# A streaming encoder step: sums of squares a k-tile per place, later first queries, four cosine buffers, w_out tiles written early, and rows of the second pair in another order

## The chip, the cores and the metric

The kernel runs on one core of one Trainium2 chip. The metric is the device time of one execution in microseconds, and the median over the runs is what counts. The engines are PE (matmul, with PEld for its weight loads), DVE (vector), ACT (scalar, with tables for functions such as Exp), POOL, and SP, which here only issues transfers.

## The reference

One inference step of a one-layer encoder on 2048 frames of a new stream and 64 frames of a running one, all in float32:

```
xn = rmsnorm(x, norm_mix);  proj = xn @ w_in              # 1024 -> 5632
x_rnn, y_gate, q, k, v, g_rnn, g_attn = split(proj)
xc = causal_dwconv(x_rnn);  h = rg_lru(xc)                # gates, then a scan over the frames
y_rnn = h * gelu(y_gate)
y_attn = window attention(rope(q), rope(k), v, sinks)     # 16 heads, 4 key heads, chunks of 64
x = x + (sigmoid(g_rnn)*y_rnn + sigmoid(g_attn)*y_attn) @ w_out
up = rmsnorm(x, norm_ffn) @ w_up;  gate, val = split(causal_dwconv(up))
x = x + (silu(gate) * val) @ w_down;  y = rmsnorm(x, norm_final)
```

Caches (keys, values, the recurrent state and the last rows of both convolutions) are outputs too.

## The kernel before

Channels lie on partitions and the 2112 tokens (2048 and 64) along the free dimension. A float32 product is made of three matmuls on a high and a low part of each operand (`mm3`, L237 to L239: `xh` and `xl` against the weight pair `whl`). `split` (L204, L205) makes such a pair: ACT rounds to the high part, then DVE subtracts for the low part, so the low part waits for ACT. `split2` and `put2` (L209, L210) do the same and return the low part as a call to be made later.

**Phase 1** (to about 1350 us) works on three sets of two token blocks (320, 384 and 352 columns a block). A set goes through the 44 tiles of w_in, 48 matmuls a tile (8 k-tiles, 3 parts, 2 blocks), into three PSUM banks in turn. In set 0, `kept` loads a tile as plain float32 (`wraw`, 512 KB, issued by SP at L226), splits it into `whl`, and POOL writes the pair to DRAM (`wiS`); sets 1 and 2 load the pairs. `wraw` has two slots and, through `fw.extend`, a third in a region `FX`.

A set begins with the projections of the queries and then of the keys, each followed by `rope` for either block (L375 to L381 on DVE, which read two PSUM banks). `trig` (L395, L396) loads the cosines and sines of a block into tiles named `h`, two of them. The results go to DRAM (`qS`, `kS`), from where attention reads them. Four groups follow, one per key head. In a group, `rnn` goes through 18 places (j = 0 to 17) of projections, gates, scan and gelu for two channel tiles (conv L623 and L628, gates L652 to L655, gelu's eviction L688, L699 to L721), and at each place one step of `attention` is taken beside it: a unit loads its queries (D and E, L539), makes scores S (L547, L548), a softmax (L550 to L565, Exp on ACT at L559), transposes `pt` of the probabilities with their split into `ph` and `pl`, and the product Y (L580, L581).

The next set's input norm is made beside groups 2 and 3 of a set. `stats` loads 8 k-tiles for each of two blocks (L255), squares them on ACT (L257, L259) and adds them up on POOL (L260); `finish` later sums over partitions with a matmul. Both blocks' 16 loads and squares are written at one place, g = 2, j = 8. `behind()` places what is written in it behind the last weight load.

**Phase 2** (to about 1565 us) multiplies by w_out for three pairs of blocks. `wload` loads 48 half tiles: the first 16 raw, the rest as pairs that were kept in DRAM (`RE<-woS`, L438). `mixes` loads the operands of the next pair (`FW<-mixS`, L411), through SP too. **Phases 3 and 4** are the feed-forward, with seven products in place of eight for each 2 by 2 square of quarters; ORDER lists the products' operands. `x1prep` makes the operands T1, 21 and 22 of the second pair from x after phase 2 (loads L909, scale L916, difference L925, then `put2`). It runs as one of the things taken beside the products. Where a quarter's product is ready, L1206 and L1208 add it up out of PSUM on DVE, which frees the bank.

Until `tc.manual_schedule()` (in front of phase 3) a scheduler chooses the order of the instructions on each engine; behind it the order is the one written.

Of the kernel before, what the change touches and what calls it, by code (L numbers as in the profile page):

```python
# [7 lines left out]
F32 = mybir.dt.float32  # L8
F32R = mybir.dt.float32r
AF = mybir.ActivationFunctionType  # L10
ALU = mybir.AluOpType
# [3 lines left out]
P = 128  # L15
T = 2112
TP = 2048
KO = 8
# [3 lines left out]
SETS = [[(0, 320), (320, 320)], [(640, 384), (1024, 384)], [(1408, 352), (1760, 352)]]  # L22
BN = 384
# [103 lines left out]
def kernel(ctx: ExitStack, tc: tile.TileContext, xT, w_in, w_out, w_up, w_dn, gw, pk,  # L127
                             sinks, cq, sq, ck, sk, kcT, vcT, kcn, vcn, augk, auge, ident_in,
                             yT, kpT, ksT, vpT, vsT, kc_o, vc_o, h_o, lc_o, fc_o):
    nc = tc.nc  # L130
# [116 lines left out]
        xblocks[t0] = (pool.tile([P, KO, BN], F32R, name="xh", bufs=2), pool.tile([P, KO, BN], F32R, name="xl", bufs=2))  # L247
        return xblocks[t0]

    def stats(t0, n):  # L250
        r = fw.tile([P, BN], F32, name="nr", bufs=2)[:, :n]
        s = fw.tile([P, BN], F32, name="ns", bufs=2)[:, :n]
        for k in range(KO):
            x = fw.tile([P, BN], F32, name="xk", bufs=4)[:, :n]
            nc.sync.dma_start(x, xT[k * P:(k + 1) * P, t0:t0 + n])  # L255
            if k == 0:
                nc.scalar.activation(s, x, AF.Square)  # L257
            else:
                nc.scalar.activation(x, x, AF.Square)  # L259
                nc.gpsimd.tensor_tensor(s, s, x, op=ALU.add)  # L260

        def finish():
            p = pmm.tile([P, 512], F32, name="mm")
            nc.tensor.matmul(p[:, :n], ones, s, start=True, stop=True)
            nc.scalar.activation(r, p[:, :n], AF.Sqrt, scale=1.0 / 1024, bias=epst)
            nc.vector.reciprocal(r, r)
            rstd[t0] = r
        return finish

    def apply(blocks):  # L270

# [67 lines left out]
        consts()  # L339

    es1 = ExitStack()

    FX = Region(tc, "FX", 4096, F32, "right")
    es1.callback(FX.close)
    fw.regions = (FW, FX)
    fw.extend("wraw", KO * P, 1)
    ap = es1.enter_context(tc.tile_pool(name="ap", bufs=1, reuse_waits="tile", side="right"))
    rp_ = es1.enter_context(tc.tile_pool(name="rp", bufs=2, reuse_waits="tile", side="right"))
    pat = es1.enter_context(tc.tile_pool(name="pat", bufs=1, space=PSUM))
# [40 lines left out]
            nc.sync.dma_start(qS[i, r0:r0 + 128, tt], t[:, :n].bitcast(F32))  # L390

    def trig(c, s, r, tt, n):
        ct = rp_.tile([P, BN], F32, name="h")
        st = rp_.tile([P, BN], F32, name="h")
        nc.sync.dma_start(ct[:r, :n], c[:, tt])  # L395
        nc.sync.dma_start(st[:r, :n], s[:, tt])  # L396
        return ct, st
# [33 lines left out]
    def wload(j):  # L431

        if j < 16:
            wraws[j] = raws.tile([P, 4 * P], F32, name="wraw")
            nc.sync.dma_start(wraws[j], w_out[j // 2][:, j % 2 * 4 * P:(j % 2 + 1) * 4 * P])
        elif j < 48:
            weights[j] = wh.tile([P, 2, 4 * P], F32R, name="wh")
            nc.sync.dma_start(weights[j].bitcast(F32), wpart(j))  # L438
# [12 lines left out]
    for si, blocks in enumerate(SETS):  # L451
# [285 lines left out]
        for g in range(4):  # L737
            kv = key_prep(g)
            ya = ap.tile([P, 2, SN], F32, name="ya")
            rr = [rp_.tile([P, SN], F32, name=f"rr{i}", bufs=1) for i in range(2)]  # L740
            ta = [[], []]
            at = attention(g, kv)
            for j, _ in enumerate(rnn(g, rr, ta)):
                next(at, None)
                if j == 3:
                    while pending:
                        pending.pop(0)()
                if g == 2 and j == 8 and si + 1 < len(SETS):
                    with behind():
                        nxt = [stats(t0, n) for t0, n in SETS[si + 1]]  # L750
                if g == 3 and j == 6:
                    for f in nxt:
                        f()
                if g == 3 and nxt:

                    if j == (16 if si == 0 else 8):
                        ahead = apply(SETS[si + 1])
                    if j in ((16, 17) if si == 0 else (9, 13, 15)):
                        with behind():
                            next(ahead)  # L760
            if g == 3 and nxt:
                for _ in ahead:
                    pass
            if g == 1 and si == 2:

                fw.close()
                xk, raws = Pool(FW), Pool(FW, right=True)
                xk.reserve("xk", BS, 16)
                raws.reserve("wraw", 4 * P, 2)
                mixed = mixes(0, xk)  # L770
                with behind():
                    next(mixed)
                    wload(0)
                    wload(1)
            if g == 3 and si == 2:

                es0.close()
                RA = Region(tc, "RA", 58368, F32R)
                mixp, wh0 = [Pool(RA), None, None], Pool(RA)
                wh0.reserve("wh", 8 * P, 4)  # L780
            for _ in at:
                if g == 3 and si == 2:
                    next(mixed)
                    next(mixed)
                    next(mixed)
            for i in range(2):
                pending.append(lambda i=i, rr=rr, ta=ta, ya=ya, g=g, blocks=blocks, s0=s0:
                               mix(2 * g + i, rr[i], ta[i], ya[:, i], blocks, s0))
# [107 lines left out]
    def x1prep(p, rs, tp):  # L896

        (t0, n), (t1, _) = PAIRS[p]
        for o in ("T1", "21", "22"):
            operand(p, o)  # L900
        where = {"11": (0, t0), "12": (0, t1), "21": (4, t0), "22": (4, t1)}
        todo = [(o, k) for k in range(4) for o in ("12", "11")] + [(o, k) for o in ("21", "22") for k in range(4)]
        raw, low = [], []

        def load(j):
            if j < len(todo):
                half, t = where[todo[j][0]]
                raw.append(tp.tile([P, n], F32, name="x1", bufs=8))
                nc.sync.dma_start(raw[j], x1S[todo[j][1] + half, :, t:t + n])  # L909

        for j in range(8):
            load(j)
        yield
        for j, (o, k) in enumerate(todo):
            half, t = where[o]
            nc.vector.scalar_tensor_tensor(raw[j], raw[j], col("g2", k + half), rs[t], op0=ALU.mult, op1=ALU.mult)  # L916
            while low:
                low.pop(0)()
                load(len(raw))
                if j < 10:  # L920
                    load(len(raw))
            if o == "12":
                continue
            if o == "11":
                nc.vector.tensor_tensor(raw[j], raw[j - 1], raw[j], op=ALU.subtract)  # L925
                o = "T1"
            low.append(put2(p, o, k, raw[j]))
            yield
        low.pop()()
# [16 lines left out]
    def wout(i, m, beside):  # L946

        work = [(t0, n, xres.pop((t0, m)), acc()) for t0, n in phases[i]]
        for j in (16 * i + 2 * m, 16 * i + 2 * m + 1):
# [9 lines left out]
                    nc.tensor.matmul(ps[:, :n], w[:, 1, c], x[:, k, 0], start=False, stop=k == 7)  # L959
            wsplit(j + 2)  # L960
            while wnext[0] < 48 and wnext[0] <= j + 4:
                wload(wnext[0])
                wnext[0] += 1
            beside()
        return work
# [430 lines left out]
    for i in range(3):  # L1396
# [14 lines left out]
        for m in range(8):  # L1411
# [17 lines left out]
            if i == 0 and m == 5:  # L1429
                drive(side, 99)  # L1430
                xk.close()
                xk = Pool(FW, right=True)
                xk.reserve("xk", BM, 3)
                side, pace = [mixes(2, xk)], (1, 0)
# [437 lines left out]
```

## Time and profile before

| | us |
|---|---|
| median of 3 runs | 2969.44 |
| lowest and highest | 2962.66, 2976.83 |
| profiled execution | 2964.2 |
| its span | 2962.4 |
| mean granted clock of PE | 0.983 |

Times in the profile are counted from the start of the span. A row of the time line has the start, the length, engine, line, operation, tiles (out<-in) and, in brackets, how long the engine had been idle and what released it. Where the prediction speaks of a wait of PE, it is such a bracket.

### The profile page before, as it was taken

Reading aid. Unit: us, or ns where it says so; the run is one execution under the profiler, and the core shown is the slowest. Engines: PE = TensorE matmul, PEld = TensorE weight load, DVE = VectorE, ACT = ScalarE, POOL = GpSimd, SP = SyncE. Lnnn points to the kernel's source line nnn. Section 1 sums busy time; section 2 is a strip of 40 time slices with the busy share of each in tenths; the row PEclk is TensorE's granted clock in tenths of the full one; section 3 lists DMA queues with packets and bytes.
Section 4 is the critical chain, followed back from the end, with each engine's and each line's share of the span. In section 5 each row is a group of like instructions: output and inputs, shape, how many; then the busy total and the mean of one; then the engine's idle time right before and its main releaser. Section 6 shows DMA issues by size and latency. Waiting matters only on the chain.

```text
span 2962.4 us, 48650 instructions
## 1 busy us (share of the span) xinstructions
PE 2856.2 (96%) x17572; PEld 2749.1 (93%) x17572; DVE 2037.4 (69%) x3998; ACT 1507.7 (51%) x3353; POOL 400.6 (14%) x699
## 2 busy tenths in 40 slices
PE   7999899999999999998898999999899999999998
PEld 6899899999999999998898999999799999999997
DVE  6388784467686277776567988888756557656686
ACT  4377772466654266665324555555544444333442
POOL 2012100000200000002321323333111111000011
PEclk8999999999999999999999999999999999999999
DMA  7867656644455745436875656565766666977573
GB/s 250 282 210 229 193 198 226 193 149 135 152 162 169 244 141 182 147 125 247 274 234 178 219 195 220 200 221 201 259 202 219 215 223 210 278 208 223 162 231 112
DMA packets 337042, 601.13 MB, mean 203 GB/s; under 512 B 39216, under 2 KB 236832, under 8 KB 319904
## 3 DMA queue, kind: packets, MB, share of 16 engines
q1 hardware_dynamic: 288096, 409.28, 44.9%
q0 software_dynamic: 48704, 188.73, 16.8%
q8 instruction: 139, 2.28, 0.3%
q14 instruction: 103, 0.84, 0.1%
HBM read 398.11 MB, written 200.29 MB: 202 GB/s over the span
## 4 chain that ended last, share of the span: by engine, by line
PE 61%; issue 15%; DVE 10%; DMA 8%; ACT 3%; POOL 2%; SPq 0%; POOLq 0%; DVEq 0%; ACTq 0%
PE mm L237 9%; PE mm L239 9%; PE mm L238 9%; PE mf L1157 3%; PE mf L1159 3%; PE mf L1158 3%; PE mf L1678 2%; PE mf L1677 2%; PE mf L1679 2%; DMA x1S<-FW 2%; PE mm L1159 2%; PE mm L1157 2%; PE mm L1158 2%; PE pt L572 2%; DMA FW<-in_xT_dram 1%
## 5 line engine op out<-in xcount | busy, mean ns | idle before, releaser
L237 PE MATMUL mm<-xh,whl 128*128 128x320 f32 (+2 forms) x2112 | 691.1, 327 | 12.6 <-DVE y L379 9.6
L238 PE MATMUL mm<-xl,whl 128*128 128x320 f32 (+2 forms) x2112 | 687.2, 325 | 5.4 <-DVE xl L205 4.7
L239 PE MATMUL mm<-xh,whl 128*128 128x320 f32 (+2 forms) x2112 | 685.9, 325 | 0.0
L209 ACT ACTIVATE RE<-FW 128x512 fp32r<-128x512 f32 (+2 forms) x540 | 288.0, 559 | 398.9 <-DVE FW L1036 98.2
L210 DVE TENSOR_TENSOR RE<-FW,RE 128x512 fp32r<-128x512 f32 (+2 forms) x540 | 313.4, 602 | 161.1 <-ACT RE L209 156.1
L237 PEld LDWEIGHTS mm<-xh,whl 128*128 128x128 f32 x2112 | 401.7, 190 | 19.7 <-DVE y L379 11.1
L238 PEld LDWEIGHTS mm<-xl,whl 128*128 128x128 f32 x2112 | 401.8, 190 | 12.2 <-DVE xl L205 8.0
L239 PEld LDWEIGHTS mm<-xh,whl 128*128 128x128 f32 x2112 | 401.4, 190 | 0.8
L1193 DVE SCALAR_TENSOR_TENSOR FA<-FA,pkt 128x608 f32<-128x608 f32 (+1 forms) x264 | 245.4, 950 | 51.1 <-ACT FA L1187 46.5
L1157 PE MATMUL mf<-RA,RE 128*128 128x304 f32 (+1 forms) x604 | 198.9, 329 | 12.5 <-ACT FW L1202 5.5
L1159 PE MATMUL mf<-RA,RE 128*128 128x304 f32 (+1 forms) x604 | 198.1, 328 | 0.0
L1158 PE MATMUL mf<-RA,RE 128*128 128x304 f32 (+1 forms) x604 | 197.5, 327 | 0.0
L1677 PE MATMUL mf<-RE 128*128 128x304 f32 (+1 forms) x594 | 192.9, 325 | 1.8 <-DVE RR L1722 1.8
L1678 PE MATMUL mf<-RE 128*128 128x304 f32 (+1 forms) x594 | 192.7, 324 | 0.6 <-DVE RE L210 0.5
L1679 PE MATMUL mf<-RE 128*128 128x304 f32 (+1 forms) x594 | 191.2, 322 | 0.0
L1158 PE MATMUL mf<-RE 128*128 128x304 f32 (+1 forms) x484 | 158.3, 327 | 4.1 <-DVE RE L210 4.1
L550 DVE TENSOR_REDUCE mx<-S 128x4 f32<-128x1024 f32 (+1 forms) x68 | 81.0, 1191 | 117.9 <-PE S L548 117.9
L1157 PE MATMUL mf<-RE 128*128 128x304 f32 (+1 forms) x484 | 158.3, 327 | 3.1 <-ACT RE L209 3.1
L1187 ACT ACTIVATE FA<-FA,pkt 128x608 f32<-128x608 f32 (+1 forms) x132 | 128.1, 970 | 64.0 <-DVE FA L1208 59.5
L1159 PE MATMUL mf<-RE 128*128 128x304 f32 (+1 forms) x484 | 158.2, 327 | 0.0
L559 ACT ACTIVATE pr<-S,nm 128x256 f32<-128x256 f32 (+1 forms) x272 | 124.0, 467 | 27.9 <-DVE nm L553 27.3
L1157 PEld LDWEIGHTS mf<-RA,RE 128*128 128x128 f32 x604 | 114.8, 190 | 17.8 <-ACT FW L1202 6.1
(335 smaller groups left out, 6954.7 us busy)
## 6 DMA issues: line engine op xcount, KB each, us to landing
whl<-wiS SPq DMA_DIRECT2D x88, 1024.0 KB, 5.3
wiS<-whl POOLq DMA_DIRECT2D x44, 1024.0 KB, 6.9
wuS<-RE POOLq DMA_DIRECT2D x88, 512.0 KB, 4.0
RE<-wuS SPq DMA_DIRECT2D x88, 512.0 KB, 4.4
FW<-in_w_up_dram SPq DMA_DIRECT2D x154, 256.0 KB, 4.1
hS<-FA POOLq DMA_DIRECT2D x154, 152.0 KB, 3.8
FW<-hS SPq DMA_DIRECT2D x154, 152.0 KB, 3.8
FW<-in_w_in_dram SPq DMA_DIRECT2D x44, 512.0 KB, 5.3
```

The costliest lines, as they stand in the source:

```text
L209: lastact[0] = nc.scalar.activation(hi, src, AF.Copy)
L210: return lambda: nc.vector.tensor_tensor(lo, src, hi.bitcast(F32), op=ALU.subtract)
L237: nc.tensor.matmul(ps[:, :n], wh[:, c], xh[:, k, :n], start=first, stop=False)
L238: nc.tensor.matmul(ps[:, :n], wh[:, c], xl[:, k, :n], start=False, stop=False)
L239: nc.tensor.matmul(ps[:, :n], wl[:, c], xh[:, k, :n], start=False, stop=last)
L1157: nc.tensor.matmul(ps[:, :n], w[:, 0, c], x[:, k, 0], start=first, stop=False, **more)
L1158: nc.tensor.matmul(ps[:, :n], w[:, 0, c], x[:, k, 1], start=False, stop=False, **more)
L1159: nc.tensor.matmul(ps[:, :n], w[:, 1, c], x[:, k, 0], start=False, stop=last, **more)
L1193: nc.vector.scalar_tensor_tensor(uc, G[:, j:j + self.cols], col("fw", 44 * j + m), uc, op0=ALU.mult, op1=ALU.add)
L1677: nc.tensor.matmul(ps[m][:, cs], w[:, 0, c], t[:, 0], start=k == 0, stop=False)
L1678: nc.tensor.matmul(ps[m][:, cs], w[:, 0, c], t[:, 1], start=False, stop=False)
L1679: nc.tensor.matmul(ps[m][:, cs], w[:, 1, c], t[:, 0], start=False, stop=k == 10)
```

## The change

`stats` becomes a generator that takes one square a place: two loads are issued ahead, and each step then squares one k-tile, adds it, and issues one load. It is stepped from g = 2, j = 4 to g = 3, j = 4. In the first group of set 0 attention starts two places later and takes two steps at j = 7 and j = 13. `trig`'s tiles have four buffers. The region `FX`, and with it the third slot of `wraw`, is gone. In phase 2, `wload(16)` to `wload(20)` are written at m = 5 of the first pair, and `wout` skips what is loaded already. `x1prep` loads four pieces ahead in place of eight, keeps up to six ahead of the piece in work, and makes the low part of the piece before ahead of the next scale.

```diff
--- before.py
+++ after.py
@@ -247,25 +247,39 @@
         xblocks[t0] = (pool.tile([P, KO, BN], F32R, name="xh", bufs=2), pool.tile([P, KO, BN], F32R, name="xl", bufs=2))
         return xblocks[t0]
 
-    def stats(t0, n):
-        r = fw.tile([P, BN], F32, name="nr", bufs=2)[:, :n]
-        s = fw.tile([P, BN], F32, name="ns", bufs=2)[:, :n]
-        for k in range(KO):
-            x = fw.tile([P, BN], F32, name="xk", bufs=4)[:, :n]
-            nc.sync.dma_start(x, xT[k * P:(k + 1) * P, t0:t0 + n])
-            if k == 0:
-                nc.scalar.activation(s, x, AF.Square)
-            else:
-                nc.scalar.activation(x, x, AF.Square)
-                nc.gpsimd.tensor_tensor(s, s, x, op=ALU.add)
-
-        def finish():
+    def stats(blocks, done):
+
+        todo = [(t0, n, k) for t0, n in blocks for k in range(KO)]
+        raw = []
+
+        def load(j):
+            if j < len(todo):
+                t0, n, k = todo[j]
+                raw.append(fw.tile([P, BN], F32, name="xk", bufs=4)[:, :n])
+                nc.sync.dma_start(raw[j], xT[k * P:(k + 1) * P, t0:t0 + n])
+
+        def finish(t0, n, r, s):
             p = pmm.tile([P, 512], F32, name="mm")
             nc.tensor.matmul(p[:, :n], ones, s, start=True, stop=True)
             nc.scalar.activation(r, p[:, :n], AF.Sqrt, scale=1.0 / 1024, bias=epst)
             nc.vector.reciprocal(r, r)
             rstd[t0] = r
-        return finish
+
+        load(0)
+        load(1)
+        yield
+        for j, (t0, n, k) in enumerate(todo):
+            x = raw[j]
+            if k == 0:
+                r = fw.tile([P, BN], F32, name="nr", bufs=2)[:, :n]
+                s = fw.tile([P, BN], F32, name="ns", bufs=2)[:, :n]
+                nc.scalar.activation(s, x, AF.Square)
+                done.append(lambda t0=t0, n=n, r=r, s=s: finish(t0, n, r, s))
+            else:
+                nc.scalar.activation(x, x, AF.Square)
+                nc.gpsimd.tensor_tensor(s, s, x, op=ALU.add)
+            load(j + 2)
+            yield
 
     def apply(blocks):
 
@@ -339,11 +353,6 @@
         consts()
 
     es1 = ExitStack()
-
-    FX = Region(tc, "FX", 4096, F32, "right")
-    es1.callback(FX.close)
-    fw.regions = (FW, FX)
-    fw.extend("wraw", KO * P, 1)
     ap = es1.enter_context(tc.tile_pool(name="ap", bufs=1, reuse_waits="tile", side="right"))
     rp_ = es1.enter_context(tc.tile_pool(name="rp", bufs=2, reuse_waits="tile", side="right"))
     pat = es1.enter_context(tc.tile_pool(name="pat", bufs=1, space=PSUM))
@@ -390,8 +399,8 @@
             nc.sync.dma_start(qS[i, r0:r0 + 128, tt], t[:, :n].bitcast(F32))
 
     def trig(c, s, r, tt, n):
-        ct = rp_.tile([P, BN], F32, name="h")
-        st = rp_.tile([P, BN], F32, name="h")
+        ct = rp_.tile([P, BN], F32, name="h", bufs=4)
+        st = rp_.tile([P, BN], F32, name="h", bufs=4)
         nc.sync.dma_start(ct[:r, :n], c[:, tt])
         nc.sync.dma_start(st[:r, :n], s[:, tt])
         return ct, st
@@ -741,13 +750,19 @@
             ta = [[], []]
             at = attention(g, kv)
             for j, _ in enumerate(rnn(g, rr, ta)):
-                next(at, None)
+
+                if (si, g) != (0, 0) or j > 1:
+                    next(at, None)
+                if (si, g) == (0, 0) and j in (7, 13):
+                    next(at, None)
                 if j == 3:
                     while pending:
                         pending.pop(0)()
-                if g == 2 and j == 8 and si + 1 < len(SETS):
+                if g == 2 and j == 4 and si + 1 < len(SETS):
+                    squares_ = stats(SETS[si + 1], nxt)
+                if si + 1 < len(SETS) and (g == 2 and j > 3 or g == 3 and j < 5):
                     with behind():
-                        nxt = [stats(t0, n) for t0, n in SETS[si + 1]]
+                        next(squares_, None)
                 if g == 3 and j == 6:
                     for f in nxt:
                         f()
@@ -908,17 +923,16 @@
                 raw.append(tp.tile([P, n], F32, name="x1", bufs=8))
                 nc.sync.dma_start(raw[j], x1S[todo[j][1] + half, :, t:t + n])
 
-        for j in range(8):
+        for j in range(4):
             load(j)
         yield
         for j, (o, k) in enumerate(todo):
+            while low:
+                low.pop(0)()
+            while len(raw) < min(j + 6, len(todo)):
+                load(len(raw))
             half, t = where[o]
             nc.vector.scalar_tensor_tensor(raw[j], raw[j], col("g2", k + half), rs[t], op0=ALU.mult, op1=ALU.mult)
-            while low:
-                low.pop(0)()
-                load(len(raw))
-                if j < 10:
-                    load(len(raw))
             if o == "12":
                 continue
             if o == "11":
@@ -959,7 +973,8 @@
                     nc.tensor.matmul(ps[:, :n], w[:, 1, c], x[:, k, 0], start=False, stop=k == 7)
             wsplit(j + 2)
             while wnext[0] < 48 and wnext[0] <= j + 4:
-                wload(wnext[0])
+                if wnext[0] not in weights:
+                    wload(wnext[0])
                 wnext[0] += 1
             beside()
         return work
@@ -1429,6 +1444,9 @@
             if i == 0 and m == 5:
                 drive(side, 99)
                 xk.close()
+
+                for j in range(16, 21):
+                    wload(j)
                 xk = Pool(FW, right=True)
                 xk.reserve("xk", BM, 3)
                 side, pace = [mixes(2, xk)], (1, 0)
```

How the orders on the engines move is shown at three places; line numbers of the changed kernel are 9 to 19 higher.

PE in the first group of set 0, before: the first row is the 24th projection matmul behind the five transposes of V (L526).

```order
L239 MATMUL mm<-xh,whl 128x320
L547 MATMUL S<-kA,D 128x128
L237 MATMUL mm<-xh,whl 128x320
L238 MATMUL mm<-xl,whl 128x320
L239 MATMUL mm<-xh,whl 128x320
L237 MATMUL mm<-xh,whl 128x320
L238 MATMUL mm<-xl,whl 128x320
L548 MATMUL S<-kB_274,E_286 128x128
L547 MATMUL S<-kA,D 128x128
```

The same place after; the first row here is the 71st projection matmul behind the transposes.

```order
L238 MATMUL mm<-xl,whl 128x320
L239 MATMUL mm<-xh,whl 128x320
L556 MATMUL S<-kA,D 128x128
L557 MATMUL S<-kB_270,E_282 128x128
L556 MATMUL S<-kA,D 128x128
L557 MATMUL S<-kB_270,E_282 128x128
L556 MATMUL S<-kA,D 128x128
L557 MATMUL S<-kB_270,E_282 128x128
L556 MATMUL S<-kA,D 128x128
```

The scores of the first unit (S, from keys kA and queries D, then kB and E) stand 48 projection matmuls later, and the eight of them are in one piece.

ACT in group 2 of set 0, about the two evictions of gelu's input (y<-mm), before. The squares are L259, on tiles in FW and FX; whl<-FW is the high part of a w_in tile.

```order
L259 ACTIVATE FX<-FX 128x384
L623 ACTIVATE xc<-mm,pkt 128x320
L628 ACTIVATE xr<-mm 128x320
L204 ACTIVATE whl<-FW 128x1024
L259 ACTIVATE FW<-FW 128x384 x2
L688 ACTIVATE y<-mm 128x320
L204 ACTIVATE xch<-xc 128x320
L670 ACT_TABLE_LOAD
L670 ACTIVATE y<-y 128x320
L259 ACTIVATE FW<-FW 128x384
L259 ACTIVATE FX<-FX 128x384
L688 ACTIVATE y<-mm 128x320
```

The same place after, where a square is L279.

```order
L632 ACTIVATE xc<-mm,pkt 128x320
L637 ACTIVATE xr<-mm 128x320
L204 ACTIVATE whl<-FW 128x1024
L279 ACTIVATE FW<-FW 128x384 x2
L697 ACTIVATE y<-mm 128x320
L204 ACTIVATE xch<-xc 128x320
L679 ACT_TABLE_LOAD
L679 ACTIVATE y<-y 128x320
L697 ACTIVATE y<-mm 128x320
```

Five squares stood ahead of the two evictions in this piece, and two do now, both ahead of the first one.

DVE in the feed-forward, before, on the last pieces of x1prep for the second pair: the scale is L916, the low part is L210 with RE<-FA; L210 with RE<-FW belongs to a tile of w_up.

```order
L1206 TENSOR_TENSOR FA<-mm,FA 128x304
L916 SCALAR_TENSOR_TENSOR FA<-FA,pkt,FW 128x304
L210 TENSOR_TENSOR RE<-FA,RE 128x304
L916 SCALAR_TENSOR_TENSOR FA<-FA,pkt,FW 128x304
L210 TENSOR_TENSOR RE<-FA,RE 128x304
L916 SCALAR_TENSOR_TENSOR FA<-FA,pkt,FW 128x304
L210 TENSOR_TENSOR RE<-FA,RE 128x304 x2
L210 TENSOR_TENSOR RE<-FW,RE 128x512
L1036 TENSOR_TENSOR FW<-FW 128x512
L1208 TENSOR_TENSOR FA<-mf,FA 128x304 x2
```

The same place after (scale L935).

```order
L1221 TENSOR_TENSOR FA<-mm,FA 128x304
L210 TENSOR_TENSOR RE<-FA,RE 128x304
L935 SCALAR_TENSOR_TENSOR FA<-FA,pkt,FW 128x304
L210 TENSOR_TENSOR RE<-FA,RE 128x304
L935 SCALAR_TENSOR_TENSOR FA<-FA,pkt,FW 128x304
L210 TENSOR_TENSOR RE<-FA,RE 128x304
L935 SCALAR_TENSOR_TENSOR FA<-FA,pkt,FW 128x304
L210 TENSOR_TENSOR RE<-FA,RE 128x304
L210 TENSOR_TENSOR RE<-FW,RE 128x512
L1051 TENSOR_TENSOR FW<-FW 128x512
L1223 TENSOR_TENSOR FA<-mf,FA 128x304 x2
```

Before, a scale stood between a piece's own scale and its low part; now the low part follows its scale directly.

## The prediction

> **What bounds the kernel now.** I read the page first, then the tensor engine's waits, then stretches of the time line around each wait.
>
> ```profile
> span 2962.4 us, 48650 instructions
> PE 2856.2 (96%) x17572; PEld 2749.1 (93%) x17572; DVE 2037.4 (69%) x3998; ACT 1507.7 (51%) x3353; POOL 400.6 (14%) x699
> ```
>
> PE is busy 2856.2 of 2962.4 us, so all that scheduling can win lies in 106 us of idle PE, plus what a slowed PE loses after a pause. Since the change leaves the products as they are, each edit is worth the PE wait it takes away or makes. The PE's waits (by line waited at and releaser: total us, times, longest):
>
> ```profile
> PE mm L237 <- DVE y L379: 9.6, 5, 3.6
> PE mf L957 <- DMA RE<-woS: 7.2, 1, 7.2
> PE mm L652 <- ACT y L688: 5.8, 2, 3.6
> PE S L547 <- ACT pr L559: 1.5, 1, 1.5
> PE mm L652 <- ACT tr L655: 1.4, 2, 1.0
> PE Y L581 <- DVE pl L205: 4.5, 6, 2.3
> PE mm L237 <- ACT ta L475: 1.2, 1, 1.2
> ```
>
> The waits are single events of 1 to 7 us. A pause costs more than its length, as five windows show (length, then busy us of PE, PEld, DVE, ACT, POOL, then the granted clock, DMA share, GB/s):
>
> ```profile
> 132.20:140.20 8.00, 7.76 (x29) 7.38 (x30) 1.36 (x5) 2.84 (x10) 0.00 (x0) 0.50 0.76 205
> 309.60:316.00 6.40, 6.39 (x27) 6.20 (x28) 3.17 (x12) 5.93 (x15) 0.57 (x1) 0.62 0.75 248
> 470.80:474.60 3.80, 3.78 (x13) 3.78 (x14) 2.94 (x6) 1.05 (x2) 0.00 (x0) 0.59 0.47 157
> 776.00:782.00 6.00, 6.00 (x19) 5.91 (x19) 2.94 (x10) 1.81 (x7) 0.57 (x1) 0.50 0.07 22
> 942.00:947.00 5.00, 4.06 (x25) 4.07 (x26) 3.66 (x8) 0.99 (x2) 0.00 (x0) 1.00 0.77 279
> ```
>
> The first four stretches follow pauses that are worked on below, and the granted clock in them is 0.50 to 0.62; a stretch of length L at clock c loses L(1-c): 4.0, 2.4, 1.6 and 3.0 us. After the pause that ends at 942.94 it is 1.00: nothing.
>
> The Trainium skill ("TensorE: Matmul & The Clock Gate", Part 1) has PE drop to half rate after an idle window of about 3.4 us and come back after about 3.4 us of work. The trace differs: 2.88 us of idle time at 470.82 was followed by 0.59, and after 5.21 us the half clock lasted 8.0 us. By the page only the pauses of 5.21 and 3.59 us would pay, 1.7 us each, and the sum below would be about 8 us smaller (2952); the measured windows decide.
>
> **The change part by part.**
>
> *Later first queries.* The first S matmul of set 0:
>
> ```profile
> 132.22 0.45 PE L547 MATMUL S<-kA,D 128*128 128x128 f32 x1 [5.21 <-DMA D<-qS]
> 134.32 0.47 PE L548 MATMUL S<-kB,E 128*128 128x128 f32 x1 [0.22 <-DMA E<-qS]
> 117.00:127.00 10.00, 10.00 (x69) 9.48 (x67) 3.84 (x5) 2.38 (x5) 1.07 (x2) 1.00 1.00 387
> ```
>
> PE stands still from 127.0 until D lands. In the new order 48 more projection matmuls stand ahead of it, at 10.00/69 = 0.145 us each: 7.0 us, so S is reached at 134.0. SP's order of the loads is the same, so D (132.2) is there and E (134.3) costs about 0.5. Gain 5.2 + 4.0 - 0.5 = **8.7**. The later softmax is covered by the projections between first and second unit (60 matmuls, 8.7 us).
>
> *Four buffers of cosines.* Now block 1's cosines reuse block 0's two buffers, and SP issues them behind queries:
>
> ```profile
> 59.26 0.48 DVE L376 TENSOR_TENSOR xc<-mm,h 32x320 f32<-32x320 f32 x1 [2.52 <-DMA h<-in_sk_dram]
> 469.24 0.56 DVE L375 TENSOR_TENSOR y<-mm,h 128x384 f32<-128x384 f32 x1 [7.15 <-DMA h<-in_cq_dram]
> 470.82 0.44 PE L237 MATMUL mm<-xh,whl 128*128 128x384 f32 x1 [2.88 <-DVE y L379]
> 940.49 0.53 DVE L375 TENSOR_TENSOR y<-mm,h 128x352 f32<-128x352 f32 x1 [3.50 <-DMA h<-in_cq_dram]
> 942.94 0.43 PE L237 MATMUL mm<-xh,whl 128*128 128x352 f32 x1 [2.06 <-DVE y L379]
> ```
>
> With four, the first key pair of set 0 and both query pairs of sets 1 and 2 are issued ahead of the query writes, the latter during the set before. DVE's waits here are for these loads alone; without them it hands its PSUM bank back in time. Gain 1.2 (the L475 wait) + 2.88 + 1.6 + 2.06 = **7.7** (bounds 5, if the clock and the key part stay, and 7.7). Nothing else is issued for it.
>
> *Squares one per place.* Now 16 loads and 16 Squares are issued in one place of the third group, and they stand on ACT ahead of evictions that PE waits for:
>
> ```profile
> 303.21 0.52 ACT L259 ACTIVATE FW<-FW 128x384 f32<-128x384 f32 x1 [1.81 <-DMA FW<-in_xT_dram]
> 303.64 0.42 ACT L688 ACTIVATE y<-mm 128x320 f32<-128x320 f32 x1
> 304.11 0.57 PE L652 MATMUL mm<-xch,gh 128*128 128x320 f32 x1 [3.59 <-ACT y L688]
> 763.47 1.54 POOL L260 TENSOR_TENSOR FW<-FW,FX 128x352 f32<-128x352 f32 x1
> 773.83 0.50 PE L581 MATMUL Y<-pl,vv 128*128 128x512 f32 x1 [2.33 <-DVE pl L205]
> ```
>
> Set 0: PE waits 5.8 for y at L688 (two waits, above) and 1.0 for tr, with 2.4 of clock: 9.2 us. The square at 303.21 waits 1.81 for its load and holds the eviction at 303.64 behind it. Two squares still stand ahead of this eviction, with loads issued behind a weight load; an estimate from that 1.81 for what stays is 2.2; gain **7** (bounds 4, if the first wait stays whole with its clock, and 9.2). Set 1: DVE is held by the POOL adds (below), and PE waits 2.33 for pl, 1.5 for pr, 0.4 for tr, with 3.0 of clock: 7.2. Spread out, one add still meets a step of the chain, 0.6 (below); gain **6.6** (bounds 2, if pl alone goes, and 7.2).
>
> *Two raw buffers in set 0 for three.* A w_in tile's load waits for the split of the tile two before it, not three:
>
> ```profile
> FW<-in_w_in_dram SPq DMA_DIRECT2D x44, 512.0 KB, 5.3
> 123.22 0.41 PE L237 MATMUL mm<-xh,whl 128*128 128x320 f32 x1
> 436.83 0.40 PE L237 MATMUL mm<-xh,whl 128*128 128x320 f32 x1
> ```
>
> The two matmuls begin w_in tiles 12 and 43: 313.6/31 = 10.1 us a tile, 20.2 for two. A load of 5.3 (9 at worst) and a split of 3 to 5 fit: cost 0 (bounds 0 and 3).
>
> *Kept weights early.* The PE waits 7.2 us for the load of w_out tile 21, issued here:
>
> ```profile
> 1408.72 19.11 SPq L411 DMA_DIRECT2D FW<-mixS  x9
> ```
>
> The five loads that the edit writes earlier (16 to 20) stood there already: SP's, PE's and DVE's orders in this stretch are the same before and after. The load of tile 21 is still behind these nine mixS loads and four more. Gain **0**.
>
> *Second pair's last rows.* Now a piece's scale (L916) is followed on DVE by the previous piece's low part (L210), so ACT's rounding in between is hidden:
>
> ```profile
> 1579.10:1599.00 19.90, 14.20 (x97) 13.45 (x97) 19.32 (x43) 9.43 (x23) 1.08 (x2) 0.97 0.62 198
> 1595.08 0.46 DVE L210 TENSOR_TENSOR RE<-FA,RE 128x304 fp32r<-128x304 f32 x1
> 1595.46 0.52 DVE L916 SCALAR_TENSOR_TENSOR FA<-FA,pkt,FW 128x304 f32<-128x304 f32 x1
> 1595.91 1.08 DVE L210 TENSOR_TENSOR RE<-FA,RE 128x304 fp32r<-128x304 f32 x2
> 1596.02 0.46 ACT L209 ACTIVATE RE<-FA 128x304 fp32r<-128x304 f32 x1 [0.37 <-DVE FA L916]
> 1598.23 0.85 DVE L1208 TENSOR_TENSOR FA<-mf,FA 128x304 f32<-128x304 f32 x2
> 1598.75 0.62 PE L1157 MATMUL mf<-RD,RE 128*128 128x304 f32 x1 [3.63 <-DVE FA L1208]
> ```
>
> Two pieces are 0.83 us apart (1595.08 and 1595.91). In the new order the low part comes next on DVE, and must wait for ACT: from L916's start to its own low part's start is 1.06 (1595.46 to the second of the pair at 1595.91, some 1596.5), then 0.39 until the next scale: 1.45 a piece. Of the eight pieces of rows 21 and 22 two have other work in between; six times 0.62 is 3.7. Three sums of the row before cost 0.4 each. DVE is busy in nearly all of the 19.9 us up to 1599 (third busy number of the first row), and the L1208 that PE waits for stands behind it all: it comes **4.9** later, and the wait grows from 3.6 to 8.5. Bounds: -3.6 (the wait goes, should the first pieces start sooner by that much) and 6.2 (all eight at 0.62, and the three sums); the rows of DVE itself give 4.9.
>
> Sum: -8.7 - 7.7 - 7 - 6.6 + 4.9 = **-25.1**. The profiled execution took 2964.2 (span 2962.4 and 1.8 around it), so it would take 2939.1. It lies 5.2 below the median of the runs, 2969.44, and the forecast is 2969.4 - 25.1 = **2944**.
>
> **The rivals.**
>
> *The squares' price comes back.* POOL's adds slow DVE wherever they stand:
>
> ```profile
> 761.63 0.96 DVE L666 SCALAR_TENSOR_TENSOR a<-t,tr 128x768 f32<-128x768 f32 x1
> 762.62 1.58 DVE L667 SCALAR_TENSOR_TENSOR a<-a,tr 128x768 f32<-128x768 f32 x1
> ```
>
> Beside an add the same shape takes 1.58 for 0.96. There are 28 adds; 28 x 0.62 is 17 us of DVE. If 13.6 of it reach PE, the squares' gain of 13.6 is gone: 2958. Against it: DVE is idle in 31% of the span. The Trainium skill ("SBUF — State Buffer", two separate sides) calls this pair of ports an exclusive lock under which the loser fully blocks; the trace shows 0.6 us lost, not the whole add's 1.54.
>
> *The rows' edit is free or better.* If the order costs nothing, 2939. If it even frees the product early, the 3.63 goes as well: 2936. For it: fewer loads stand ahead of the first scale. Against it: DVE has no pause to fill there.
>
> *Kept weights do what their name says.* Were tile 21's load issued with the five, its 7.2 us would go: 2937. The equal orders speak against it.
>
> *Slower than before: two raw buffers bind set 0.* Load and split of a tile in one buffer must fit two tiles of PE, 20.2 us. Now they take 8 to 14; from 20.2 it decides. At 23, 15 pairs times 2.8 add 42: 2986. Against it: it would need loads more than twice as long.
>
> **How the numbers follow.** The forecast as worked out (2936 to 2953): 0.65. Squares' price back (2958): 0.14. Rows free or better (2936 to 2939): 0.13. Kept weights work: 0.02. Raw buffers bind: 0.04. Small mixed losses near 2965: 0.02. Range 2930 to 2960: it takes in the bounds of squares (+8) and rows (-8.5, +1.3) with those of set 0's buffers and cosines (+3 each), and the first rival; about 1 in 10 lies above it. A measurement tells 0.5% (14.8 us) from no change. Below 2954.6 is faster: 0.78; slower, above 2984.3, is 0.05; between them 0.17.
>
> **What would show it.** Right: the waits for D, in_cq, in_sk and y L688 gone from PE's list, clock 1.00 behind them; the woS wait still 7 us; the wait for FA L1208 near 8 us. Wrong: new waits in the third and fourth group with POOL's adds beside DVE's chain, PE waiting for splits of w_in in set 0, or an L1208 wait that is no longer than now.

## The result and the profile after

| | before | after |
|---|---|---|
| median of 6 runs (us) | 2966.57 | 2948.26 |
| lowest and highest | 2962.0, 2976.83 | 2937.76, 2955.39 |
| ratio, 95% interval | | 0.994, 0.9921 to 0.996 |
| profiled execution | 2964.2 | 2955.39 |
| its span | 2962.4 | 2953.6 |
| PE reaches the first wait of phase 2 (its 5.01 us for RA) at | 1354.35 | 1330.83 |
| the last short wait behind the quarters' sums (0.47, 0.48) at | 1663.55 | 1646.45 |
| from the 3.94 us wait ahead of phase 4 to the end of the span | 819.5 | 828.4 |

The median fell by 18.3 us against a forecast of 25.1. The time lies inside the forecast's range, but the interval of the ratio leaves a gain of 12 to 23 us, less than was forecast. The profiled execution of the changed kernel is the slowest of its six, so its span alone (8.8 us less) understates the change; the three rows at the foot show where: 23.5 us won in phase 1, 6.4 given back until 1646, and 8.9 in phase 4, which the change does not touch.

The page of the changed kernel, and its waits of PE (line and releaser: total, times, longest):

```profile
span 2953.6 us, 48667 instructions
PE 2855.2 (97%) x17572; PEld 2744.5 (93%) x17572; DVE 2038.3 (69%) x3998; ACT 1510.2 (51%) x3355; POOL 401.5 (14%) x699
```

```profile
PE mf L971 <- DMA RE<-woS: 8.1, 1, 8.1
PE mf L1172 <- DVE FA L1223: 6.7, 2, 6.5
PE mm L237 <- DVE y L388: 4.7, 3, 3.7
PE mf L1172 <- ACT FA L1217: 4.0, 2, 2.6
PE Y L590 <- DVE pl L205: 3.3, 5, 1.3
PE mm L661 <- ACT y L697: 3.0, 3, 1.8
PE mm L237 <- ACT ta L494: 2.5, 1, 2.5
```

The wait for D is gone, that for DVE's y (L379, now L388) fell from five times to three, and that for pr (L559, now L568) is gone. The wait for woS stayed, the wait for the sum (L1208, now L1223) grew from 3.6 to 6.5, and the wait for ta (L485, now L494) from 0.9 to 2.5. In the time line of PE, and in a window (the granted clock is the last number but two):

```profile
84.70 0.41 PE L237 MATMUL mm<-xh,whl 128*128 128x320 f32 x1 [2.47 <-ACT ta L494]
293.81 0.41 PE L661 MATMUL mm<-xch,gh 128*128 128x320 f32 x1 [0.67 <-ACT y L697]
296.27 0.41 PE L661 MATMUL mm<-xch,gh 128*128 128x320 f32 x1 [1.76 <-ACT y L697]
298.48 0.64 PE L661 MATMUL mm<-xch,gh 128*128 128x320 f32 x1 [1.50 <-ACT tr L664]
1547.13 0.62 PE L1172 MATMUL mf<-RA,RE 128*128 128x304 f32 x1 [6.56 <-ACT RE L209]
1581.80 0.62 PE L1172 MATMUL mf<-RD,RE 128*128 128x304 f32 x1 [6.52 <-DVE FA L1223]
```

```profile
297.50:304.00 6.50, 5.52 (x19) 5.33 (x20) 2.90 (x9) 6.03 (x17) 0.53 (x1) 0.50 1.03 356
```

At gelu's evictions in set 0 the pauses fell from 6.8 to 3.9 us, but the clock in this window, which begins inside the last of them, is 0.50: half clock followed as it did behind the longer ones. And x1prep's low parts wait for ACT one by one, as forecast; DVE of the changed kernel:

```profile
1570.15 0.47 DVE L210 TENSOR_TENSOR RE<-FA,RE 128x304 fp32r<-128x304 f32 x1 [0.53 <-ACT RE L209]
1570.54 0.53 DVE L935 SCALAR_TENSOR_TENSOR FA<-FA,pkt,FW 128x304 f32<-128x304 f32 x1
1571.59 0.48 DVE L210 TENSOR_TENSOR RE<-FA,RE 128x304 fp32r<-128x304 f32 x1 [0.52 <-ACT RE L209]
```

A piece takes 1.44 us (1570.15 to 1571.59), for which 1.45 was forecast.

### The profile page after: what moved, and what is told of

Its sections match the earlier page's. It is cut to its first block, busy times and chain, and to the rows that moved or that the text cites. A ratio compares the mean times of both kernels' runs of the same rounds, so it can differ in the third digit from the quotient of the medians.

```text
span 2953.6 us, 48667 instructions
## 1 busy us (share of the span) xinstructions
PE 2855.2 (97%) x17572; PEld 2744.5 (93%) x17572; DVE 2038.3 (69%) x3998; ACT 1510.2 (51%) x3355; POOL 401.5 (14%) x699
## 4 chain that ended last, share of the span: by engine, by line
PE 61%; issue 15%; DVE 10%; DMA 7%; ACT 4%; POOL 2%; SPq 0%; DVEq 0%; POOLq 0%; ACTq 0%
PE mm L237 9%; PE mm L239 9%; PE mm L238 9%; PE mf L1172 3%; PE mf L1174 3%; PE mf L1173 3%; PE mf L1696 3%; PE mf L1695 2%; PE mf L1697 2%; PE mm L1174 2%; PE mm L1172 2%; PE mm L1173 2%; PE pt L581 2%; DMA FW<-in_xT_dram 1%; POOL hS L1247 1%
## 5 line engine op out<-in xcount | busy, mean ns | idle before, releaser
L210 DVE TENSOR_TENSOR RE<-FW,RE 128x512 fp32r<-128x512 f32 (+2 forms) x540 | 313.3, 602 | 168.5 <-ACT RE L209 165.8
L1208 DVE SCALAR_TENSOR_TENSOR FA<-FA,pkt 128x608 f32<-128x608 f32 (+1 forms) x264 | 245.3, 950 | 53.1 <-ACT FA L1202 48.4
L559 DVE TENSOR_REDUCE mx<-S 128x4 f32<-128x1024 f32 (+1 forms) x68 | 81.0, 1191 | 98.1 <-PE S L557 98.1
L568 ACT ACTIVATE pr<-S,nm 128x256 f32<-128x256 f32 (+1 forms) x272 | 124.0, 467 | 28.7 <-DVE nm L562 28.0
```

What stands on the lines that cost most here:

```text
L210: return lambda: nc.vector.tensor_tensor(lo, src, hi.bitcast(F32), op=ALU.subtract)
L1208: nc.vector.scalar_tensor_tensor(uc, G[:, j:j + self.cols], col("fw", 44 * j + m), uc, op0=ALU.mult, op1=ALU.add)
```

## The experiments

The ratios are to the kernel of before, run on the same chip in the same session. Since single effects are of 3 to 13 us and the runs of one kernel spread over 7 to 22, I read them from waits and from the moment at which PE reaches the same instruction, and take the ratios for the whole. "End of phase 1" below is the start of the wait for RA, 1330.83 in the changed kernel.

**e1: kept weights undone.**

```diff
-                for j in range(16, 21):
-                    wload(j)
```

> The changed kernel with the edit of the kept weights undone (tiles 16 to 20 of w_out written where they were). Theory: the edit moved nothing, the instruction orders of all engines are those of the changed kernel; ratio to before 0.994 as the changed kernel has, PE's wait for the load of tile 21 (DMA RE<-woS) stays at 7 to 8 us, and any difference to the changed kernel's profile is what two executions of one program differ by (I expect the 128x448 matmuls of the feed-forward to run at 203 ns here or at 207 ns, by chance). Rival: the early loads matter; then the wait for RE<-woS changes by more than 2 us.

Measured: 2944.09 us, ratio 0.9939 (0.9919 to 0.9958). The instruction order of every engine is that of the changed kernel, and the wait for woS is 10.1 us here. That is 2.1 us from the changed kernel's 8.1, which was the rival's sign, but with equal orders it is a difference between two executions. So the edit is worth nothing, and this is a second profile of the same program. It shows what the phase 4 of the first one hid. Three windows of 100 us, of before, after and e1:

```profile
2250.00:2350.00 100.00, 100.00 (x495) 92.69 (x494) 60.10 (x89) 45.64 (x114) 11.32 (x21) 1.00 0.64 217
```

```profile
2250.00:2350.00 100.00, 100.00 (x486) 90.83 (x485) 59.47 (x86) 43.80 (x112) 9.70 (x18) 1.00 0.63 219
```

```profile
2250.00:2350.00 100.00, 100.00 (x495) 92.67 (x494) 61.55 (x89) 45.21 (x114) 10.31 (x20) 1.00 0.63 217
```

PE is busy throughout at a granted clock of 1.00 in all three, and yet makes 495, 486 and 495 matmuls. Start to start, a 128x448 matmul takes 202.7 ns or 206.7 ns, for hundreds of us on end.

**e2: x1prep as before.**

```diff
-        for j in range(4):
+        for j in range(8):
             load(j)
...
-            while low:
-                low.pop(0)()
-            while len(raw) < min(j + 6, len(todo)):
-                load(len(raw))
             half, t = where[o]
             nc.vector.scalar_tensor_tensor(raw[j], ...)
+            while low:
+                low.pop(0)()
+                load(len(raw))
+                if j < 10:
+                    load(len(raw))
```

> The changed kernel with x1prep as before. Theory (my forecast): the new order of low parts costs; PE's wait for DVE FA at the sum of the quarter (L1223 in the changed kernel) falls from 6.5 to about 3.6 us, the two waits for ACT FA ahead of it from 1.3 and 2.6 to about 0.9 and 1.2, so some 5 us are won, ratio about 0.992. The wait for ACT RE of 6.6 us ahead of them is a slow landing of w_up and should be 4 to 7 either way. Rival: the order is free and the growth comes from elsewhere; then these waits stay at 6.5, 1.3 and 2.6.

Measured: 2943.22 us, ratio 0.9937 (0.9916 to 0.9959), which the runs cannot tell from the changed kernel. The waits in the time line of PE can:

```profile
1566.27 0.41 PE L1173 MATMUL mf<-RA,RE 128*128 128x304 f32 x1 [0.89 <-ACT FA L1218]
1571.06 0.42 PE L1173 MATMUL mf<-RA,RE 128*128 128x304 f32 x1 [1.16 <-ACT FA L1218]
1581.64 0.41 PE L1173 MATMUL mf<-RD,RE 128*128 128x304 f32 x1 [3.61 <-DVE FA L1224]
```

0.89, 1.16 and 3.61 in place of 1.33, 2.63 and 6.52: 4.8 us, and with the slowed clock behind them 5.9 (13.3 to 7.4). In the eight profiles with the new order PE's waits at these sums add up to 9.6 to 10.8 us, in the six with the old one to 5.7 to 6.7. The order costs about what the forecast said.

**e3: first queries early again** (attention taken from j = 0 in every group, no double steps).

> The changed kernel with attention in the first group of set 0 taken from j = 0, as before. Theory: PE waits again some 5 us for the load of D, with half clock behind it, about 8 to 9 us in all; ratio about 0.997. Rival: D would come earlier now because the key cosines come earlier; then the wait is under 3 us.

Measured: 2949.62 us, ratio 0.9957 (0.9943 to 0.9972). PE's time line:

```profile
130.96 0.45 PE L556 MATMUL S<-kA,D 128*128 128x128 f32 x1 [4.74 <-DMA D<-qS]
```

4.74 us and 3.9 of clock come back at the place, 8.6 in all. Yet phase 1 ends only 3.1 later than in the changed kernel, mostly since the waits at 67 and 82 us, which with their clock took 4.8 there, happen to take 0.8 here.

**e4: squares together** (all of them at g = 2, j = 8).

```diff
-                if g == 2 and j == 4 and si + 1 < len(SETS):
-                    squares_ = stats(SETS[si + 1], nxt)
-                if si + 1 < len(SETS) and (g == 2 and j > 3 or g == 3 and j < 5):
+                if g == 2 and j == 8 and si + 1 < len(SETS):
                     with behind():
-                        next(squares_, None)
+                        for _ in stats(SETS[si + 1], nxt):
+                            pass
```

> The changed kernel with all squares of the next set at g = 2, j = 8 again (two raw w_in buffers, four cosine buffers as changed). Theory: set 1 shows again waits of PE for pl and pr of 4 to 5 us with 3 us of slowed clock between 720 and 760 us, and set 0 waits at gelu's evictions of 6 to 7 us in place of 3.9; 8 to 11 us lost, ratio about 0.997. Rival (POOL's adds cost as much wherever they stand): no difference, 0.994.

Measured: 2953.07 us, ratio 0.9977 (0.9962 to 0.9992), phase 1 ends at 1343.87, 13.0 later. The waits of PE are back in both sets:

```profile
300.04 0.62 PE L661 MATMUL mm<-xch,gh 128*128 128x320 f32 x1 [3.75 <-ACT y L697]
303.21 0.63 PE L661 MATMUL mm<-xch,gh 128*128 128x320 f32 x1 [2.02 <-ACT y L697]
307.93 0.79 PE L589 MATMUL Y<-ph,vv 128*128 128x512 f32 x1 [3.55 <-ACT ph L204]
751.33 0.39 PE L556 MATMUL S<-kA,D 128*128 128x256 f32 x1 [1.54 <-ACT pr L568]
768.48 0.51 PE L590 MATMUL Y<-pl,vv 128*128 128x512 f32 x1 [2.34 <-DVE pl L205]
```

The pauses in set 1 are those of before, but no slowed clock follows them, where 3 us were expected (see the last section).

The rival that POOL's adds cost as much wherever they stand falls. Spread out, one of them meets DVE's chain in set 1 of the changed kernel, and PE waits 0.54 us:

```profile
712.37 1.06 POOL L280 TENSOR_TENSOR FW<-FW 128x352 f32<-128x352 f32 x1 [9.04 <-ACT FW L279]
712.73 1.58 DVE L709 TENSOR_TENSOR y<-y,tr 128x384 f32<-128x384 f32 x2
715.58 0.30 PE L581 MATMUL pt<-ident,pr 128*128 128x128 f32 x1 [0.54 <-DVE pr L574]
```

In e4, where no add runs beside it, the same pair of L709 takes 1.01 us and the 0.54 is not there.

**e5: the next set's query cosines held back** behind a weight load of the fourth group.

```diff
-            ct, st = trig(cq, sq, P, tt, n)
+            with tc.issue_after(hold[0].ins) if hold else nullcontext():
+                ct, st = trig(cq, sq, P, tt, n)
...
                 if g == 3 and j == 6:
+                    hold[:] = [lastw[0]]
```

> The changed kernel with the next set's query cosines held back until the weight loads of the fourth group (four buffers stay). Theory: in the changed kernel set 1's cosines are issued at 57 to 68 us, among set 0's key writes; the wait of DVE for kS<-y (5.3 us near 64) and PE's waits at 67 (0.7) and 82 us (2.5, with 1.6 of clock) come from that. Held back, DVE waits for kS<-y about 1 us as before the change, PE waits at 82 us about 1 us, and at 451 to 470 and 911 to 941 us nothing new appears: 3 to 4 us won. Rival: the wait at 82 us is the landing of kr<-kS, which varies by itself (0.8 to 4.6 us in the four runs with early cosines so far); then it stays above 2 us though the wait for kS<-y goes.

Measured: 2943.34 us, ratio 0.9927 (0.9899 to 0.9955). The waits at 67 and 82 us are gone, but DVE still waits 3.8 us for kS<-y at 62 us, so that part of the theory falls: the writes of the keys are slow without the cosines too. What goes is the wait for kr, the keys read back. What was won is lost later; PE:

```profile
418.21 0.80 PE L592 MATMUL Y<-pl,vv 128*128 128x512 f32 x1 [4.66 <-DVE pl L205]
```

DVE waits 4.3 us there for a load of x, which the scaling of the next set's input needs (L300), and pl stands behind it. The load was issued at 409.01 and took 6.7 us to land; the same load took 2.3 to 3.5 us in the thirteen other profiles. The held cosines were not in its way, as SP issued the last of them by 341 and all had landed by 346. Why it was late is open; with an earlier hold (e9) the wait at this place is 0.8.

**e6: squares' loads three ahead** (`load(2)` in front, `load(j + 3)` in the loop).

> The changed kernel with the squares' loads three ahead in place of two. Theory: the three waits of PE at 293 to 298 us (3.9 us and 2.6 of clock) come from two squares that wait 2.6 us for their loads and hold the eviction behind them; with one more load ahead these waits fall to under 2 us in all and the clock stays up: 4 us won. Rival: the fourth load only waits for its buffer behind the same squares, and nothing changes.

Measured: 2945.51 us, ratio 0.9947 (0.9927 to 0.9966). The rival's outcome holds: PE waits 0.31, 1.75 and 1.50 us there, with 2.8 of clock. The loads stand behind a weight load by `behind()`, whatever their number, and ACT still waits for one ahead of the eviction (ACT's time line):

```profile
292.08 0.52 ACT L280 ACTIVATE FW<-FW 128x384 f32<-128x384 f32 x1 [1.24 <-DMA FW<-in_xT_dram]
```

**e7: kept w_out tiles from 21 on through POOL** (`(nc.sync if j < 21 else nc.gpsimd).dma_start`).

> The changed kernel with the kept w_out tiles from 21 on loaded through POOL's queue. Theory: PE's wait of 7 to 10 us for tile 21 is SP's queue (the load stands behind thirteen loads of mixS that wait for their buffers); through POOL it is issued once tile 16 is used up, the wait falls under 2 us, and with its clock 8 to 10 us are won, ratio about 0.991. Rival: POOL's queue holds it behind the writes of x1S, or the load waits for its buffer; then the wait stays above 5 us.

Measured: 2945.22 us, ratio 0.9944 (0.9925 to 0.9963). The wait is 5.2 us, with two more of 2.8 and 1.5 behind it: the rival. POOL's queue shows the load behind writes of x1S, and issued at 1408.49:

```profile
1407.31 1.07 POOL L985 DMA_DIRECT2D x1S<-FW  x2
1408.49 1.44 POOL L447 DMA_DIRECT2D RE<-woS  x2
```

**e8: the kernel of before with two raw w_in buffers** (region FX left out).

> The kernel of before with region FX left out: two raw w_in buffers, and squares of the next set in FW alone. Theory: set 0 does not need the third buffer; the first 280 us keep before's waits (127 us: 5.2) and no wait of PE for a split of w_in appears, ratio 1.000 within 0.002. Rival: load plus split exceed two tiles of PE; waits of 1 to 3 us per pair of tiles appear between 50 and 440 us.

Measured: 2970.53 us, ratio 1.0031 (1.0015 to 1.0047), outside what was expected. But phase 1 ends at 1354.15 (before: 1354.35), with no new wait for a split; its 128x448 matmuls took 206.7 ns. Set 0 does not need the third buffer. The ratio may come from that spacing; this is not shown, since only one of its runs has a profile.

**e9: three things mended:** x1prep as in e2, cosines held back from group 1 on (`if g == 1 and j == 6`), and no square at two places:

```diff
-                if si + 1 < len(SETS) and (g == 2 and j > 3 or g == 3 and j < 5):
+                if si + 1 < len(SETS) and (g == 2 and j > 3 and j not in (9, 10) or g == 3 and j < 5):
```

> The changed kernel with three things mended: x1prep as before; the next set's query cosines held back only to the second group; and no square at places 9 and 10 of the third group, so that none stands ahead of gelu's evictions there. Theory: the waits of PE at 293 to 298 us (3.9 us and 2.6 of clock) go, since only the two squares with late loads held the eviction; the waits at 67 and 82 us stay away as in the run with cosines held, without that run's new wait near 413 us; the waits at the quarter's sum are 0.9, 1.2 and 3.6 us. Some 15 us less than the changed kernel in the phases up to 1650 us, ratio about 0.989. Rival for the squares: the evictions wait for something else there, and the waits stay; then 8 us less.

Measured: 2939.07 us, ratio 0.9911 (0.9894 to 0.9927), with e10's the lowest of all. PE at gelu's evictions:

```profile
291.97 0.41 PE L663 MATMUL mm<-xch,gh 128*128 128x320 f32 x1 [0.95 <-ACT y L699]
294.18 0.63 PE L663 MATMUL mm<-xch,gh 128*128 128x320 f32 x1 [1.51 <-ACT tr L666]
```

The waits for y fell from 2.4 to 0.95, so the two squares made most of them; the rest and the wait for tr, of 1.5, stay and are not the squares' doing. The wait at 82 us is 0.6, and the sums wait 0.9, 1.2 and 3.6. Up to the last wait of the quarters it is 10.1 us ahead of the changed kernel (1636.37 against 1646.45), not the 15 expected, and 4.5 of this is the landing of w_up, for which PE waits 2.1 here and 6.6 there.

**e10: mixS of the third pair through POOL as well** (`(nc.gpsimd if i == 2 else nc.sync).dma_start` in `mixes`).

> The kernel of e9 with the loads of mixS for the third pair issued through POOL's queue, so that SP holds only loads of x1S ahead of w_out tile 21. Theory: SP's thirteen waiting loads are what makes tile 21 late; PE's wait of 7 to 10 us for it falls under 3 us, ratio about 0.986. Rival: the loads of x1S that then stand ahead wait as long, or the tile's buffer comes free no earlier; the wait stays above 5 us and the ratio is that of e9.

Measured: 2941.53 us, ratio 0.9911 (0.9891 to 0.9932). The wait grew to 12.7 us: without the mixS loads, three loads of x1S stand ahead of tile 21 and wait (1404.02 to 1411.69).

**e11: two cosine buffers.**

> The changed kernel with two cosine buffers. Theory: DVE waits again for in_cq at both set boundaries and PE with it, 2.9 us with 1.6 of clock near 459 us and 2.1 near 917 us; at 60 us the wait of 1.2 for the key cosines is back and those at 67 and 82 us are as before the change (0 and 1 to 2); 3 to 6 us lost, ratio about 0.996. Rival: the boundaries wait for something else by now; then no wait of 2 us appears there.

Measured: 2950.43 us, ratio 0.996 (0.9946 to 0.9975), phase 1 ends 8.0 later. PE's time line:

```profile
464.09 0.44 PE L237 MATMUL mm<-xh,whl 128*128 128x384 f32 x1 [3.65 <-DVE y L388]
926.78 0.42 PE L237 MATMUL mm<-xh,whl 128*128 128x352 f32 x1 [1.05 <-DVE y L388]
```

Both boundaries wait again. The wait at 60 us is not back, and the one at 82 us is 2.6.

**e12: tile 21 ahead of all on SP.** To e10's edit:

```diff
-            while wnext[0] < 48 and wnext[0] <= j + 4:
+            while wnext[0] < 48 and wnext[0] <= j + (5 if j > 15 else 4):
...
-        load(0, *where)
+        with tc.issue_after(ahead22[0].ins) if p == 0 else nullcontext():
+            load(0, *where)
```

> The kernel of e10 with w_out tile 21 written one tile of products earlier (up to five ahead from tile 16 on) and the loads of x1S held behind tile 22, so that on SP nothing stands ahead of tile 21 but its own buffer. Theory: tile 16 is used up at about 1397 us (pair 2's products begin at 1394.0 in e9 and a tile takes 3.35 us), the load is issued then, lands 4 to 8 us later, and PE, which needs it 13 us after that, waits under 1 us; 8 to 12 us and their clock are won against e9, ratio 0.987 to 0.989. Rival: some of it comes back as a wait for the operands made from x1S (now later) or for the fifth buffer; then the phases up to 1560 us gain less than 5 us.

Measured: 2937.44 us, ratio 0.9916 (0.9896 to 0.9936). SP issues tiles 21 and 22 by 1398, and the wait for tile 21 is gone, but others stand in its place (PE's waits, the last of them for a later tile):

```profile
PE mm L980 <- DVE FW L993: 5.3, 1, 5.3
PE mf L833 <- DVE FW L1002: 2.2, 1, 2.2
PE mf L980 <- DMA RE<-woS: 2.1, 1, 2.1
```

PE reaches the w_up landing at 1541.24 (1539.76 in e9): nothing won. DVE's L993 hands back PSUM banks, and stands on DVE behind splits of mixS, whose loads now come late through POOL: the last of them lands at 1421, in e9 at 1414.

## Why the prediction was right, term by term

Pauses with the clock loss behind them (at gelu's evictions, behind the last of them), in us, at each place, from one profile each:

| term | forecast | before | after | undone in the changed kernel |
|---|---|---|---|---|
| first queries | -8.7 | 9.4 | 0 | +8.6 at the place (e3) |
| cosines at the set boundaries | -6.5 | 6.6 | 0 | +6.4 (e11) |
| cosines of the keys (60, 67, 82 us) | -1.2 | 2.2 | 4.8 | not back (e11) |
| squares, set 0 | -7 | 9.2 | 6.7 | phase 1 +13.0 |
| squares, set 1 | -6.6 | 8.0 | 0.5 | with both sets (e4) |
| two raw buffers | 0 | | | 0 (e8 against before) |
| kept weights | 0 | 11.1 | 10.3 | same order (e1) |
| x1prep | +4.9 | 9.3 | 13.3 | -5.9 (e2) |

The five rows of phase 1 that moved add up to 23.4 us, of the 23.5 by which PE is ahead at its end.

**Right in mechanism and size:** the queries, the cosines at the boundaries, the raw buffers, the kept weights, and x1prep, the one edit that costs. Of x1prep the forecast put all 4.9 us into the wait for the sum (3.6 to 8.5); that wait grew to 6.5, and the rest came in two waits ahead of it (0.9 to 1.3 and 1.2 to 2.6).

**Right in mechanism, the size in part a draw: squares in set 1.** The pauses that went are 4.9 us, with a second wait for pl of 0.7 that the forecast left out, and the add that still meets the chain costs 0.5 where 0.6 was forecast. The clock loss of 3 us belongs to the one execution that was profiled: behind the same pauses it was 1.7 in e8 and nothing in e4. What an add takes from DVE is not a fixed 0.6 us either. The L667 that the prediction shows began 0.77 us before the add in the row below ended, and lost 0.62; in before and after, each of the 42 instructions of DVE that took over 0.15 us longer beside an add lost the time up to that add's end, less 0.13 to 0.20 us. So "0.6 us lost, not the whole add's 1.54" compares the loss with the wrong length.

```profile
761.85 1.54 POOL L260 TENSOR_TENSOR FW<-FW 128x352 f32<-128x352 f32 x1 [0.69 <-ACT FW L259]
```

**Mis-sized: squares in set 0.** The term that failed is the "estimate from that 1.81 for what stays is 2.2". The pauses that stayed are 3.9 us, and the price that was forgotten is the clock: 2.8 us behind pauses of 0.7, 1.8 and 1.5, where it was 2.4 behind 3.6, 2.2 and 1.0. So the gain is 2.5 and lies below the forecast's lower bound of 4, and of its signs the wait for y is not gone and the clock is not 1.00. Of the pauses 2.5 us stay with no square ahead (e9).

**Wrong: "Nothing else is issued for it." and the 1.2 at 60 us.** Four buffers let set 1's cosines be issued in the midst of set 0's keys. The wait for kr at 82 us was 0.9, 2.1 and 2.6 in the three profiles with two buffers, 0.8 to 4.6 (mean 2.9) in the seven with four, and 0 to 0.6 in the four with the cosines held back. Holding them removes it; how much of it the four buffers add, three profiles can't say. The wait at 60 us was 1.2 in one profile of three with two buffers, 0.2 and nothing in the others: the forecast priced an accident of one execution. The cosines' gain is 4.0 in all (6.6 less 2.6), below the lower bound of 5.

**Not foreseen:** the landing of w_up ahead of the quarters, 4.3 us before and 6.6 after. In twelve other profiles it is 1.8 to 7.6, in e1 7.6: it varies from execution to execution, and no part of the change is shown to move it.

The forecast of 25.1, less 4.5 at the squares of set 0 and 3.8 at the keys, with 0.9 more at set 1 and 0.9 less lost at x1prep, gives 18.6; the median fell by 18.3. That waits of single profiles come so close to a median with an interval of 12 to 23 us is luck. What else differs by a microsecond or two is within what one program's executions differ by.

## What to carry to other kernels

A pause that becomes shorter can keep its whole clock loss, so price what stays with its clock, and take the clock loss of one profile as one draw. A deeper buffer also moves transfers ahead, into whatever runs then: look at what the new early transfers meet. And a load that is late behind a queue is moved with profit only if the next work in line is ready too: tile 21's wait of 8 us was taken away and came back as a wait for DVE.

## What the runs showed of the hardware

The 128x448 matmuls ran from 2150 to some 2500 us at 202.7 ns, start to start, in six of the fourteen profiles and at 206.7 ns in eight, both at a granted clock of 1.00, and the same program showed both (after and e1). From 2650 to 2800 us all fourteen ran at 202.7. From the 3.94 us wait to the end of the span the six take 813.3 to 819.5 us (mean 816.7) and the eight 823.1 to 828.4 (mean 825.0). This 8 us is as large as most edits here. What sets it is open.

The clock loss behind a pause depends on when the pause falls. In all fourteen profiles every stretch of half clock begins on one grid of 3.41 us, fixed within an execution, and lasts one to four steps of it (the end of the span cuts the last). Behind the first 14 us, a step with under 1.1 us of idle PE was never followed by half clock, and one with 1.85 us or more always was; in between, it was in 17 of 84. So the pause of 2.06 us before 942.94 in the kernel of before cost nothing: 1.63 us of it fell into one step and 0.43 into the next. And the same pauses of 2.3 and 0.7 us in set 1 were followed by different clocks in before, e8 and e4:

```profile
776.00:782.80 6.80, 6.80 (x23) 6.71 (x24) 2.94 (x10) 1.84 (x8) 0.57 (x1) 0.55 0.06 19
```

```profile
776.40:783.20 6.80, 6.80 (x30) 6.71 (x31) 2.97 (x10) 2.33 (x8) 0.57 (x1) 0.75 0.13 29
```

```profile
770.60:777.40 6.80, 6.78 (x39) 6.74 (x40) 2.99 (x10) 2.35 (x8) 0.57 (x1) 1.00 0.29 86
```

At gelu's evictions the pauses of 0.95 and 1.5 us were followed by one step of half clock in e9, by none in e10 and by two in e12.

Pauses far under 3 us cost clock when they come close together: 0.67, 1.76 and 1.50 us within 6 us were followed by 5.5 us at 0.50 (298.48 to 304.03 in the changed kernel). The Trainium skill ("TensorE: Matmul & The Clock Gate", Part 1) speaks of an idle window of about 3.4 us; no single pause here was that long.
